# Sample streams' score tiles: the two halves of the keys side by side in place of two streams' tokens

## The chip, the cores and the metric

The kernel runs on one core of one Trainium2 chip. The metric is the device time of one execution in microseconds (us). A core has the engines PE (TensorE: matmuls and transposes, PEld is its weight load), DVE (VectorE), ACT (ScalarE), POOL (GpSimd) and SP (SyncE, which here only issues transfers); transfers run on 16 DMA engines shared by all queues.

## What is computed

Two layers over 512 prompt tokens and 8 sample streams of 16 new tokens each; layer 0 is stick-breaking attention, layer 1 gated linear attention. The change is in layer 0, in the attention of the sample streams. For one stream and one of 16 heads (head width 128) the keys are 512 cached ones followed by the stream's 16 new ones:

```python
z = einsum('bqhd,bkhd->bhqk', q, k) * SB_HEAD_DIM ** -0.5
mask = kpos[None, :] < qpos[:, None]
neg_log_keep = where(mask, softplus(z), 0.0)
between = cumsum(neg_log_keep, axis=3, reverse=True) - neg_log_keep
a = where(mask, exp(log_sigmoid(z) - between), 0.0)
o = einsum('bhqk,bkhd->bqhd', a, v)
```

So each weight is a sigmoid of its score times the product of (1 - sigmoid) over all later keys that the token may see: a running product over the keys from the last to the first.

## The kernel before

**The attention stage.** Heads are taken in 8 pairs. Per pair, q, k (head width on the partitions, tokens along the row) and v are fetched from scratch memory by `fetch_pair` (L959), two pairs held at a time. Three lanes work on them: two prompt lanes (one per head of the pair, four units of 128 queries per pair) and the sample lane (L1044), whose unit `u = (p, m)` is head pair p and the two streams 2m and 2m+1: 32 units in all.

**One unit of the sample lane.** `turned` transposes the cached keys of one stream (4 blocks for each head) on PE, and DVE or ACT copies them to `kt`. `scores` (L1076) fills a bank of 128 rows by 512 keys with four matmuls of 32 weight columns each, one for each row group j of 32 rows: group j is head j // 2 and stream j % 2, and its 32 rows are the 16 tokens of *both* streams, so that the 16 rows of the other stream are computed and never used. Four more matmuls of 32 columns put the new keys' scores in a second bank (`zn`, L1086); DVE adds a mask to it (L1087). `stick` (L939) takes two sigmoids of the 512 columns and two of the 32 on ACT (L945 to L949), and the running product on DVE as one scan over 544 columns (L952). DVE multiplies sigmoid and product (L1089 for 512 columns, L1091 for 32). `weigh` (L1095) transposes four blocks of weights (L1100) and the block of the new keys (L1103) into two banks; ACT copies the one (L1101), DVE the other (L1104). `mix` (L1107) multiplies by the values: 5 blocks of keys by 4 row groups, 20 matmuls. `leave` (L1121) transposes the result back and copies it to the pair's output. Each f32 matmul is two instructions in the trace.

**What sets the order.** PE's instructions run in the order in which they are written. That order comes from a planner at build time: a clock `pe["now"]` that advances by an estimate for each matmul, and a `Side` object (L276 to L343) whose `tick` is called between pieces of the large matrix products (`plain`, L650, and `share`, L696), which so fill PE between the lanes' steps. Each lane yields steps: an estimated wait, the number of PSUM banks of kind `tp` (4 exist here) and `z` (2 exist) that it needs free, and whether it is `tiled`, that is, uses matmuls of 32 weight columns. A step runs once its wait is over and its banks are free by the planner's own count, in which a `tp` bank is held for 2.2 us from when a step took it and a `z` bank for 3.0 us. In one tick the planner first collects the lanes that are due, runs those at an ordinary step, and then those of the same list that now stand at a tiled step, whose own wait is then not looked at again:

```python
due = [x for x in self.lanes if x[1][0] <= pe["now"]]
...
tiled = [x for x in due if x in self.lanes and x[1][2]]
if tiled and pe["now"] >= self.tiled_at + self.every:
    for x in tiled:
        if self.fits(x):
            self.run(x)
```

So `scores` of the next unit can be written right behind `weigh`, if the banks for both are free. The sample lane asks for: `turned` 2 `tp` (twice a unit), `scores` with the `mix` behind it 2 `tp` and 1 `z` (L1152; the first unit 1 `tp`), `leave` 1, `weigh` 2 (L1167), which is due 6.5 us of the planner's clock after `scores`. The other engines and the transfers are ordered by the framework; SP issues nearly all transfers, one after another, and a transfer that has to wait for its buffer holds up those behind it. Keys are fetched two units ahead into a ring of two buffers (`kc`), values one unit ahead into a ring of four (`vc`). `settle` (L980) hands a pair's output on to the output projection, and fetches the pair after the next.

Of the kernel before, what the change touches and what calls it, by code (L numbers as in the profile page):

```python
# [41 lines left out]
def hybrid_step_kernel(ctx: ExitStack, tc: tile.TileContext, A: dict, O: list):  # L42
# [22 lines left out]
    def block(x):  # L65

        pe["now"] += 0.11
        return x
# [840 lines left out]
    with tc.tile_pool(name="kp", bufs=2, reuse_waits="tile") as kp, \  # L909
# [10 lines left out]
        mask_n = at.tile([P, 32], F32, name="mask_n", bufs=1)  # L920
        nc.gpsimd.memset(mask_n, 0.0)
        for j in range(4):
            bi = j % 2
            q = mask_n[32 * j:32 * j + 32, :]
            nc.gpsimd.affine_select(out=q, in_=q, pattern=[[1, 32]], base=-16 * bi,
                                    channel_multiplier=0, compare_op=ALU.is_ge, fill=NEG)
            nc.gpsimd.affine_select(out=q, in_=q, pattern=[[-1, 32]], base=0,
                                    channel_multiplier=1, compare_op=ALU.is_gt, fill=NEG)
            if bi == 0:
                nc.gpsimd.affine_select(out=q, in_=q, pattern=[[0, 32]], base=15,  # L930
                                        channel_multiplier=-1, compare_op=ALU.is_ge, fill=NEG)
        zero_c = at.tile([P, 1], F32, name="zero_c", bufs=1)
        nc.gpsimd.memset(zero_c, 0.0)
        zeros = zero_c.to_broadcast([P, 544])
# [4 lines left out]
        def stick(kind, z, zn, n):  # L939

            w = n + (32 if zn is not None else 0)
            size = 544 if kind == "s" else 512
# [4 lines left out]
            if zn is not None:  # L947
                act(k1[:, n:w], zn, AF.Sigmoid, scale=-ZSCALE)  # L948
                act(s1[:, n:w], zn, AF.Sigmoid, scale=ZSCALE)  # L949
            nc.gpsimd.memset(k1[:, w:w + 1], 1.0)  # L950
            kr = k1[:, :w][:, ::-1]
            dve.tensor_tensor_scan(kr, kr, zeros[:, :w], 1.0, ALU.mult, ALU.add)  # L952
# [51 lines left out]
        def prompt_lane(hh):  # L1004
# [4 lines left out]
            def scores(u):  # L1009
# [6 lines left out]
                s1, k1 = stick("p", z[:, :n], None, n)  # L1016
# [27 lines left out]
        def sample_lane():  # L1044
# [4 lines left out]
            def cached(u, bi, s, tag, bufs, at=at):  # L1049
                p, m = units[u]  # L1050
                t = at.tile([P, 4, 256], F32, tag=tag, name=tag, bufs=bufs)
                src = A[s][0, 2 * m + bi].rearrange("(c p) h d -> p c (h d)", p=P)
                load(t, src[:, :, 256 * p:256 * p + 256])
                return t

            def fetch_k(u):
                if u < len(units):
                    for bi in range(2):
                        kc_t[u, bi] = cached(u, bi, "cache_sb_k", "kc", 2, kp)

            def fetch_v(u):
                if u < len(units):
                    vc_t[u] = [cached(u, bi, "cache_sb_v", "vc", 4) for bi in range(2)]

            def turned(kc):
                KTs = []
                for hh in range(2):
# [3 lines left out]
                    kt = at.tile([P, PAST], F32, tag="kt", name="kt", bufs=4)  # L1071
                    (nc.scalar.copy if hh else dve.tensor_copy)(kt, tp)
# [3 lines left out]
            def scores(u, KTs):  # L1076
                p, m = units[u]
                q, k = pairs[p][:2]
                tok = slice(NP + 32 * m, NP + 32 * m + 32)
                z, zn = bank("z"), bank("tp")  # L1080
                for j in range(4):
                    hh, bi = j // 2, j % 2
                    mm(z[32 * j:32 * j + 32, :], q[:, hh, tok], by(q[:, hh, tok], KTs[2 * bi + hh]), start=True, stop=True)  # L1083
                for j in range(4):
                    hh = j // 2
                    mm(zn[32 * j:32 * j + 32, :32], q[:, hh, tok], by(q[:, hh, tok], k[:, hh, tok]), start=True, stop=True)  # L1086
                dve.tensor_tensor(zn[:, :32], zn[:, :32], mask_n, op=ALU.add)  # L1087
                s1, k1 = stick("s", z, zn[:, :32], PAST)
# [915 lines left out]
```

## Time and profile before

| | |
|---|---|
| times of three runs | 2570.55, 2567.61, 2566.62 us; median 2567.61 |
| profiled execution | span 2566.7 us, as the fastest of the three runs |
| PE busy | 2450.5 us, 95% of the span |
| DVE / ACT / POOL busy | 1593.6 / 1015.8 / 163.6 us |
| mean granted TensorE clock | 0.979 |
| attention stage | about 936 to 1405 us of the span; the first `scores` of the sample lane at 949.6, the last at 1392.2 |

Times in a row of the trace are in us from the span's start; "mean ns" is the mean duration of one instruction. Matmuls are pipelined, so that what a group costs PE is read from the start of the group to the start of the next, not from its duration. "idle" names the time in which an engine stood before an instruction, and what ended it.

### The profile page before, as it was taken

To read this page: it belongs to the slowest core of one execution; us is meant where nothing else is said; L and a number is where in the kernel's file an instruction comes from. 1 tells how busy PE (TensorE), PEld (TensorE's weight loads), DVE (VectorE), ACT (ScalarE), POOL (GpSimd) and SP (SyncE) were. 2 spreads that over 40 slices of the span, in tenths; PEclk is the share of its full clock that TensorE was granted. 3 is DMA by queue.
4 is the path that set the end of the run, shared out by engine and by line. 5 is a ranking of instruction groups with operands and counts; after the bars stand their busy time and mean duration, and the time that the engine had idled before them with its cause. 6 is when DMAs were issued, how large, how long until landed. Compare 5 with 4: busy or idle time off the path is not lost.

```text
span 2566.7 us, 43490 instructions
## 1 busy us (share of the span) xinstructions
PE 2450.5 (95%) x17369; PEld 2156.7 (84%) x17369; DVE 1593.6 (62%) x2469; ACT 1015.8 (40%) x1794; POOL 163.6 (6%) x385
## 2 busy tenths in 40 slices
PE   6899999999999999999999989999999999979998
PEld 4589999999999998787777768999999988857776
DVE  5575655555566656666776577666767465555456
ACT  4332222222223335565444344333333464455223
POOL 0010000000000000000000000000000234342000
PEclk8999999999999999999999999999999999989999
DMA  9966666766663366766665763344444777785634
GB/s 341 330 200 222 214 205 215 231 214 195 211 197 117 121 210 204 232 214 221 215 220 176 238 197 120 107 121 138 116 115 117 209 228 246 226 281 192 207 119 144
DMA packets 452797, 502.06 MB, mean 196 GB/s; under 512 B 26090, under 2 KB 349810, under 8 KB 452466
## 3 DMA queue, kind: packets, MB, share of 16 engines
q1 hardware_dynamic: 429634, 435.55, 53.7%
q0 software_dynamic: 16048, 51.92, 6.1%
q10 hardware_dynamic: 6912, 11.80, 1.2%
q8 instruction: 137, 2.24, 0.4%
q14 instruction: 66, 0.54, 0.1%
HBM read 410.05 MB, written 89.13 MB: 194 GB/s over the span
## 4 chain that ended last, share of the span: by engine, by line
PE 76%; DMA 6%; DVE 6%; issue 2%; ACT 2%; POOL 1%; SPq 0%; ACTq 0%; POOLq 0%; DVEq 0%
PE ps_mm L592 39%; PE ps_mm L696 10%; PE ps_mm L650 6%; PE ps_mm L367 3%; PE ps_tp L1070 2%; PE ps_tp L1526 2%; PE ps_mm L516 1%; PE ps_tp L1038 1%; DMA gv<-kr 1%; PE ps_z L1014 1%; PE ps_z L180 1%; PE ps_mm L1975 1%; DVE wl L135 1%; PE ps_z L1083 1%; PE ps_tp L1115 1%
## 5 line engine op out<-in xcount | busy, mean ns | idle before, releaser
L592 PE MATMUL ps_mm<-sums,wh 128*128 128x320 f32 x2752 | 616.6, 312 | 3.8 <-ACT wh L134 3.8
L592 PEld LDWEIGHTS ps_mm<-sums,wh 128*128 128x128 f32 x2752 | 460.6, 189 | 12.9 <-issue 7.4
L592 PE MATMUL ps_mm<-h,wh 128*128 128x320 f32 x2064 | 462.5, 312 | 3.4 <-DVE u L598 3.4
L592 PE MATMUL ps_mm<-sums,wl 128*128 128x320 f32 x1376 | 427.1, 310 | 1.4 <-DVE wl L135 1.4
L135 DVE TENSOR_TENSOR wl<-wr,wh 128x1024 fp32r<-128x1024 f32 x194 | 237.2, 1224 | 241.2 <-ACT wh L134 234.8
L592 PEld LDWEIGHTS ps_mm<-h,wh 128*128 128x128 f32 x2064 | 343.6, 188 | 19.3 <-issue 13.3
L134 ACT CAST wh<-wb 128x1024 fp32r<-128x1024 f32 x170 | 178.4, 1049 | 426.6 <-PE ps_mm L592 368.6
L134 ACT CAST wh<-wr 128x1024 fp32r<-128x1024 f32 x194 | 203.6, 1050 | 335.5 <-PE ps_mm L592 185.6
L592 PE MATMUL ps_mm<-h,wl 128*128 128x320 f32 x1032 | 319.2, 309 | 0.0
L650 PE MATMUL ps_mm<-h,wh 128*128 128x320 f32 x1152 | 269.1, 321 | 8.6 <-ACT wh L134 4.1
L592 PEld LDWEIGHTS ps_mm<-sums,wl 128*128 128x128 f32 x1376 | 259.7, 189 | 1.9 <-DVE wl L135 1.9
L135 DVE TENSOR_TENSOR wl<-wb,wh 128x1024 fp32r<-128x1024 f32 x170 | 207.8, 1222 | 60.8 <-ACT wh L134 60.4
L650 PEld LDWEIGHTS ps_mm<-h,wh 128*128 128x128 f32 x1152 | 196.1, 192 | 25.6 <-issue 12.2
L696 PE MATMUL ps_mm<-wh,ogh 128*128 128x512 f32 x460 | 199.5, 434 | 5.6 <-DVE y L701 2.6
L592 PEld LDWEIGHTS ps_mm<-h,wl 128*128 128x128 f32 x1032 | 194.0, 188 | 0.0
L696 PE MATMUL ps_mm<-wh,ogl 128*128 128x512 f32 x460 | 181.5, 395 | 0.4 <-DVE ogl L135 0.4
L650 PE MATMUL ps_mm<-h,wl 128*128 128x320 f32 x576 | 180.8, 314 | 1.0 <-DVE wl L135 1.0
L696 PE MATMUL ps_mm<-wl,ogh 128*128 128x512 f32 x460 | 181.3, 394 | 0.0
L696 PEld LDWEIGHTS ps_mm<-wh,ogh 128*128 128x128 f32 x460 | 87.3, 190 | 33.4 <-issue 16.5
L650 PEld LDWEIGHTS ps_mm<-h,wl 128*128 128x128 f32 x576 | 110.6, 192 | 1.7 <-DVE wl L135 1.7
L952 DVE TENSOR_TENSOR_SCAN k<-k,zero_c 128x544 f32<-128x544 f32 (+4 forms) x96 | 93.3, 976 | 29.3 <-ACT k L948 16.6
L696 PEld LDWEIGHTS ps_mm<-wh,ogl 128*128 128x128 f32 x460 | 86.8, 189 | 20.7 <-DVE ogl L135 0.9
(352 smaller groups left out, 3773.3 us busy)
## 6 DMA issues: line engine op xcount, KB each, us to landing
ar<-in_w_ada_dram SPq DMA_DIRECT2D x160, 512.0 KB
wb<-in_sb_w_in_dram SPq DMA_DIRECT2D x82, 512.0 KB
kc<-in_cache_sb_k_dram SPq DMA_DIRECT2D x64, 512.0 KB
vc<-in_cache_sb_v_dram SPq DMA_DIRECT2D x64, 512.0 KB
wr<-in_gla_w_in_dram SPq DMA_DIRECT2D x51, 512.0 KB
wb<-in_gla_w_in_dram SPq DMA_DIRECT2D x45, 512.0 KB
wr<-in_sb_w_in_dram SPq DMA_DIRECT2D x44, 512.0 KB
ar<-in_w_ada_dram SPq DMA_DIRECT2D x64, 256.0 KB
```

The source lines that it names most:

```text
L134: nc.scalar.copy(hi, x)
L135: (e or dve).tensor_tensor(lo, x, hi.bitcast(F32), op=ALU.subtract)
L180: mm(acc[32 * q:32 * q + 32, :w], cT[:, kt + m, :], by(cT[:, kt + m, :], rs[m // each][:, m % each, q, :]), start=kt + m == 0, stop=kt + m ...
L367: mm(acc[a], l[:, c], by(l[:, c], r[:, k2, :]), start=kt == k0 and first, stop=kt == k0 + nk - 1 and last)
L516: mm(acc[a], l, by(l, r[:, e, :]), start=j == 0 and e == 0 and begun, stop=j == 7 and e == 1 and last)
L592: mm(acc, l[:, k, :], by(l[:, k, :], r), start=start and k == 0 and first, stop=k == 7 and last, skip_group_check=True)
L650: mm(acc[nt], l[:, k, :], by(l[:, k, :], r), start=k0 == 8 and k == 0 and first, stop=k0 == 0 and k == 7 and last)
L696: mm(acc, l, by(l, r[:, e, :]), start=i == 0 and e == 0 and first, stop=i == 1 and e == 1 and last)
L952: dve.tensor_tensor_scan(kr, kr, zeros[:, :w], 1.0, ALU.mult, ALU.add)
L1014: mm(z[:, :n], q[:, hh, qs], by(q[:, hh, qs], k[:, hh, :n]), start=True, stop=True)
L1070: turn_block(tp[:, P * c:P * c + P], block(kc[:, c, P * hh:P * hh + P]), ident)
L1526: mm(out, l[a], by(l[a], r[b]), start=start and n == 0, stop=stop and n == 2, skip_group_check=True)
```

## The change

In a row group of 32 rows there is now one stream and one head: rows 0 to 15 are its 16 tokens against the first 256 cached keys, rows 16 to 31 the same tokens against the last 256 and the new keys. The score tile has 256 columns of cached keys and 16 of new ones, in one bank.

- `q_one` (new tile) holds for both heads and all 8 streams 16 columns of zeros, the 16 query columns, and 16 of zeros. With the window that begins at the queries a matmul writes rows 0 to 15 and adds zero to rows 16 to 31; with the window that begins 16 earlier, the reverse. Scores are 8 matmuls of 256 columns (4 groups by 2 halves, added up in the bank) in place of 4 of 512. `fetch_q` loads `q_one` from the q scratch: two transfers of 64 KB for each pair, 128 partitions by 8 runs of 64 bytes each, the first at the start of the lane, the others behind the `scores` of a pair's last unit.
- The new keys' scores are 4 matmuls of 16 columns (before: 32), written beside the others in the same bank; their mask is 16 columns wide and lets rows 16 to 31 alone through.
- `stick` is two sigmoids of 272 columns and one scan over 272.
- The running product of the earlier half lacks the factor of the later half. A `stream_shuffle` brings each row's partner's product to it (one column), a `tensor_scalar` with the two columns of `later` turns it into 1 for the later half, and the product with the sigmoid becomes a `scalar_tensor_tensor` over 256 columns with that factor.
- The new keys' weights are written by two small multiplies (one for each stream) in place of one.
- `weigh` transposes 2 + 1 blocks into one bank, and ACT alone copies it (384 columns), to a fixed tile `aT_s`. `mix` has the same 20 matmuls; its 32 weight columns are windows that begin at row 0 or 16 of a group.
- In the planner: `scores` with `mix` asks for 1 `tp` in place of 2 (the first unit for none), `weigh` for 1 in place of 2, and is due 6.0 us after `scores` in place of 6.5.
- At the start of the stage, POOL's masks change (12 selects in place of 10), and it clears `q_one` and 16 columns of `aT_s`.

```diff
+        q_one = at.tile([P, 2, NB, 3 * NT], F32, name="q_one", bufs=1)
+        nc.gpsimd.memset(q_one, 0.0)
+        aT_s = at.tile([P, 3 * P + NT], F32, name="aT_s", bufs=1)
...
-            w = n + (32 if zn is not None else 0)
-            size = 544 if kind == "s" else 512
+            size = PAST // 2 + NT if kind == "s" else 512
...
-            if zn is not None:
-                act(k1[:, n:w], zn, AF.Sigmoid, scale=-ZSCALE)
-                act(s1[:, n:w], zn, AF.Sigmoid, scale=ZSCALE)
...
+            def fetch_q(p):
+                for hh in range(2):
+                    load(q_one[:, hh, :, NT:2 * NT], q_d[p][:, hh, NP:].rearrange("d (b t) -> d b t", b=NB))
...
-                z, zn = bank("z"), bank("tp")
-                for j in range(4):
-                    hh, bi = j // 2, j % 2
-                    mm(z[32 * j:32 * j + 32, :], q[:, hh, tok], by(q[:, hh, tok], KTs[2 * bi + hh]), start=True, stop=True)
-                for j in range(4):
-                    hh = j // 2
-                    mm(zn[32 * j:32 * j + 32, :32], q[:, hh, tok], by(q[:, hh, tok], k[:, hh, tok]), start=True, stop=True)
-                dve.tensor_tensor(zn[:, :32], zn[:, :32], mask_n, op=ALU.add)
-                s1, k1 = stick("s", z, zn[:, :32], PAST)
-                dve.tensor_tensor(s1[:, :PAST], s1[:, :PAST], k1[:, 1:PAST + 1], op=ALU.mult)
+                z = bank("z")
+                for n in range(2):
+                    for j in range(4):
+                        bi, hh = j // 2, j % 2
+                        l = q_one[:, hh, 2 * m + bi, NT - NT * n:3 * NT - NT * n]
+                        mm(z[32 * j:32 * j + 32, :256], l, by(l, KTs[j][:, n]), start=n == 0, stop=n == 1)
+                for j in range(4):
+                    bi, hh = j // 2, j % 2
+                    t0 = NP + NT * (2 * m + bi)
+                    l = q[:, hh, t0 - NT:t0 + NT]
+                    mm(z[32 * j:32 * j + 32, 256:272], l, by(l, k[:, hh, t0:t0 + NT]), start=True, stop=True)
+                dve.tensor_tensor(z[:, 256:272], z[:, 256:272], mask_n, op=ALU.add)
+                s1, k1 = stick("s", z[:, :272], 272)
+                w = at.tile([P, 1], F32, tag="w", name="w")
+                dve.stream_shuffle(w, k1[:, 0:1], [(r + 16) % 32 for r in range(32)])
+                dve.tensor_scalar(w, w, later[:, 1:2], later[:, 0:1], op0=ALU.mult, op1=ALU.add)
+                dve.scalar_tensor_tensor(s1[:, :256], s1[:, :256], w, k1[:, 1:257], op0=ALU.mult, op1=ALU.mult)
...
-                aT = at.tile([P, 5, P], F32, tag="aTs", name="aT", bufs=1)
                 tp = bank("tp")
-                for c in range(4):
+                for c in range(2):
                     turn_block(tp[:, P * c:P * c + P], block(s1[:, P * c:P * c + P]), ident)
-                nc.scalar.copy(aT[:, :4, :], tp.rearrange("p (b t) -> p b t", t=P))
-                tp = bank("tp")
-                turn_block(tp[:, :P], block(an), ident)
-                dve.tensor_copy(aT[:, 4, :], tp[:, :P])
-                made[u] = aT
+                turn_block(tp[:, 2 * P:3 * P], block(an), ident)
+                nc.scalar.copy(aT_s[:, :3 * P], tp[:, :3 * P])
+                made[u] = aT_s
...
             fetch_k(0)
+            fetch_q(0)
             fetch_v(0)
...
-                yield step(1.6, tp=1 if left or not u else 2, z=1, tiled=True)
+                yield step(1.6, tp=0 if left or not u else 1, z=1, tiled=True)
                 scores(u, KTs)
+                if m == 3 and p + 1 < NPAIR:
+                    fetch_q(p + 1)
...
-                yield step(max(0.5, made[u][2] + 6.5 - pe["now"]), tp=2)
+                yield step(max(0.5, made[u][2] + 6.0 - pe["now"]), tp=1)
```

More of the change, by code (lines that the diff above doesn't have):

```diff
@@ L1047, in sample_lane, with fetch_k @@
             made, kc_t, vc_t = {}, {}, {}
-            def cached(u, bi, s, tag, bufs, at=at):
+            def fetch_k(u):
+                if u >= len(units):
+                    return
                 p, m = units[u]
[L1051 to L1059, printed above, removed]
-            def fetch_v(u):
-                if u < len(units):
-                    vc_t[u] = [cached(u, bi, "cache_sb_v", "vc", 4) for bi in range(2)]
+                for bi in range(2):
+                    src = A["cache_sb_k"][0, 2 * m + bi].rearrange("(c p) h d -> p c (h d)", p=P)
+                    kc = kc_t[u, bi] = kp.tile([P, 4, 256], F32, tag="kc", name="kc")
+                    load(kc, src[:, :, 256 * p:256 * p + 256])
+            def fetch_q(p):
+                for hh in range(2):
+                    load(q_one[:, hh, :, NT:2 * NT], q_d[p][:, hh, NP:].rearrange("d (b t) -> d b t", b=NB))
+            def fetch_v(u):
+                if u >= len(units):
+                    return
+                p, m = units[u]
+                vc_t[u] = []
+                for bi in range(2):
+                    t = at.tile([P, 4, 256], F32, tag="vc", name="vc", bufs=4)
+                    src = A["cache_sb_v"][0, 2 * m + bi].rearrange("(c p) h d -> p c (h d)", p=P)
+                    load(t, src[:, :, 256 * p:256 * p + 256])
+                    vc_t[u].append(t)
             def turned(kc):
@@ L1070, in turned @@
                         turn_block(tp[:, P * c:P * c + P], block(kc[:, c, P * hh:P * hh + P]), ident)
-                    kt = at.tile([P, PAST], F32, tag="kt", name="kt", bufs=4)
-                    (nc.scalar.copy if hh else dve.tensor_copy)(kt, tp)
+                    kt = at.tile([P, 2, 256], F32, tag="kt", name="kt", bufs=4)
+                    (nc.scalar.copy if hh else dve.tensor_copy)(kt, tp.rearrange("p (s n) -> p s n", s=2))
                     KTs.append(kt)
@@ L1111, in mix @@
                     for j in range(4):
-                        hh, bi = j // 2, j % 2
+                        bi, hh = j // 2, j % 2
                         hc = slice(P * hh, P * hh + P)
                         rhs = V[bi][:, kb, hc] if kb < 4 else v[:, 4, hc]
-                        mm(o[32 * j:32 * j + 32, :P], aT[:, kb, 32 * j:32 * j + 32], by(aT[:, kb, 32 * j:32 * j + 32], rhs),
-                           start=kb == 0, stop=kb == 4)
+                        c0 = 32 * j + (P * (kb % 2) + NT * (kb // 2) if kb < 4 else 2 * P + NT)
+                        l = aT[:, c0:c0 + 32]
+                        mm(o[32 * j:32 * j + 32, :P], l, by(l, rhs), start=kb == 0, stop=kb == 4)
                 osb = at.tile([P, P], F32, tag="osb", name="osb")
```

39 lines of the change are left out of this document (21 added, 18 removed).

## The prediction

> **What bounds the kernel now.** I read the page first, then windows over the attention stage, then what PE waited for there.
>
> ```profile
> span 2566.7 us, 43490 instructions
> PE 2450.5 (95%) x17369; PEld 2156.7 (84%) x17369; DVE 1593.6 (62%) x2469; ACT 1015.8 (40%) x1794; POOL 163.6 (6%) x385
> PE 76%; DMA 6%; DVE 6%; issue 2%; ACT 2%; POOL 1%; SPq 0%; ACTq 0%; POOLq 0%; DVEq 0%
> ```
>
> ```profile
> 1000.00:1100.00 100.00, 93.84 (x919) 78.40 (x918) 67.44 (x140) 56.14 (x136) 1.81 (x24) 0.98 0.69 224
> 1100.00:1200.00 100.00, 100.00 (x856) 80.90 (x854) 63.66 (x127) 58.68 (x139) 1.86 (x23) 1.00 0.67 222
> 1200.00:1300.00 100.00, 97.23 (x865) 76.72 (x864) 75.61 (x149) 52.05 (x123) 1.79 (x23) 1.00 0.69 228
> ```
>
> ```profile
> PE ps_tp L1031 <- DVE s L1017: 5.4, 4, 2.7
> PE ps_tp L1070 <- DMA kc<-in_cache_sb_k_dram: 2.9, 1, 2.9
> PE ps_mm L696 <- ACT ogh L134: 2.3, 1, 2.3
> ```
>
> In a row of windows the first number after the length is PE's busy time, then PEld, DVE, ACT and POOL, the granted clock, the DMA share and GB/s. In the stage that the change touches, PE is busy 94 to 100 us of 100 at a clock of 0.98 to 1.00, DVE 64 to 76, ACT 52 to 59. The last fence has the three longest groups of PE's waits in 935 to 1410 us (total, times, longest): 5.4 us behind the prompt lanes' products on DVE, once 2.9 for keys, once 2.3 at the hand-over to `share`. So the stage is PE's own work written one after another, since `plain` and `share` fill what the lanes leave. Halving ACT's and DVE's work on the sample tiles, the larger part of the edit, hardly reaches the end; what PE no longer does counts in full, and so does each new wait of PE.
>
> **Transposes of the weights.** One `weigh` on PE, each row with its start first:
>
> ```profile
> 1255.00 0.60 PE L1100 MATMUL ps_tp<-ident,s 128*128 128x128 f32 x4
> 1255.44 0.27 PE L1103 MATMUL ps_tp<-ident,a_new 128*128 128x128 f32 x1
> ```
>
> Four transposes take 1255.44 - 1255.00 = 0.44 us, 0.11 each. Two are gone in each of 32 units: 64 x 0.11 = **-7.0 us**, on PE's path.
>
> **Scores and mix.** The block that follows it:
>
> ```profile
> 1257.93 1.06 PE L1083 MATMUL ps_z<-kt,q 128*32 128x512 f32 x8
> 1258.81 0.24 PE L1086 MATMUL ps_tp<-k,q 128*32 128x32 f32 x8
> 1258.87 1.06 PE L1115 MATMUL ps_tp<-vc,aT 128*32 128x128 f32 x32
> 1259.75 0.40 PE L1115 MATMUL ps_tp<-v,aT 128*32 128x128 f32 x8
> ```
>
> Eight instructions of 512 columns take 1258.81 - 1257.93 = 0.88 us; 32 instructions of `mix` with 128 columns, as many columns in all, also take 0.88. Four times the instructions cost nothing more, so 16 of 256 take 0.88 too: 0. The new keys' eight take 0.06; with 16 columns they lie between 0.03 and 0.06, so 0 to -1.0 us over 32 units; I take the middle, **-0.5**. `mix` keeps its 20 matmuls.
>
> The Trainium skill speaks against this: its page TensorEngine Tiling (Array Packing), section Instruction Overhead, gives each matmul some 60 cycles, and lets one with a free size of 1 take as long as one of 60. By it, and by the 2.4 GHz of the Trainium skill's page TensorE: Matmul & The Clock Gate (its table of figures), 8 more instructions would cost an estimated 8 x 60 / 2.4 = 200 ns a unit, 6.4 us in all, and the time would be 2568.4. The two equal blocks of 0.88 us above do not bear it out for groups in turn on four column tiles.
>
> **ACT and DVE.**
>
> ```profile
> L952 DVE TENSOR_TENSOR_SCAN k<-k,zero_c 128x544 f32<-128x544 f32 x32 | 41.3, 1289 | 16.7 <-ACT k L948 16.6
> L1089 DVE TENSOR_TENSOR s<-s,k 128x512 f32<-128x512 f32 x32 | 21.8, 682 | 0.0
> L952 DVE TENSOR_TENSOR_SCAN k<-k,zero_c 128x256 f32<-128x256 f32 x16 | 10.9, 685 | 1.8 <-ACT k L945 1.7
> L1017 DVE TENSOR_TENSOR s<-s,k 128x256 f32<-128x256 f32 x16 | 6.7, 422 | 0.8
> L1104 DVE COPY aT<-ps_tp 128x128 f32<-128x128 f32 x31 | 8.8, 285 | 7.7 <-PE ps_tp L1103 7.7
> L1091 DVE TENSOR_TENSOR a_new<-s,k 128x32 f32<-128x32 f32 x32 | 5.9, 185 | 0.0
> L945 ACT ACTIVATE k<-ps_z 128x512 f32<-128x512 f32 x48 | 28.8, 600 | 28.8 <-PE ps_tp L1086 17.7 <-DVE ps_z L1015 9.3 <-PE ps_z L1083 1.6
> ```
>
> DVE a unit: the scan falls from 1289 ns to a little over the 685 of 256 columns (some 720), the product from 682 to some 450 (422 for 256 columns, more for a second factor), the copy of 285 goes. Added are a second `a_new` (185), the shuffle and the small `tensor_scalar`. No row shows a shuffle; below it the least it can be is near nothing, above it the 422 ns of a product of 256 columns; I take 185 for each of the two, as the smallest row here. Sum: -570 -230 -285 + 3 x 185 = -0.5 us, 17 us over the stage (between -0.8 and -0.3 a unit). ACT saves two fifths of two sigmoids of 600 ns and the two small ones, near 1 us a unit. All this lies beside PE. It counts where PE waited for DVE: of the 5.4 us behind L1017 between 0 and all; I take **-1.5**, since most of that queue is the prompt lanes' own. The mask is now added before the sigmoids, so ACT stands at its head until DVE comes; casts of weights and copies of `kt` queue behind it. The near 1 us that it saves covers that; without this cover `turned` would wait for its bank.
>
> **The planner's order.** With one bank less asked for, `scores` will mostly be written right behind `weigh`, where it now mostly stands some 3 us later (1255.00 and 1257.93 above). Then `mix` comes 1 us behind `weigh` and can catch ACT's copy unfinished. One such place today:
>
> ```profile
> 996.60 1.06 PE L1083 MATMUL ps_z<-kt,q 128*32 128x512 f32 x8
> 997.48 0.24 PE L1086 MATMUL ps_tp<-k,q 128*32 128x32 f32 x8
> 997.76 1.08 PE L1115 MATMUL ps_tp<-vc,aT 128*32 128x128 f32 x32
> ```
>
> ```profile
> PE ps_tp L1115 <- ACT aT L1101: 1.1, 2, 0.6
> ```
>
> From L1086 to `mix` 0.28 us pass in place of 0.06. I count about 10 of 32 units so today; for 21 more, 0 to 0.22 each is 0 to +4.6. The second row (two waits, 1.1 us in all over the stage) puts the mean well under the bound, and the copy is shorter: **+1.1**. On the gain side, from 1060 to 1080 the lanes run without a large product to fill PE:
>
> ```profile
> 1060.00:1070.00 10.00, 7.41 (x94) 5.32 (x93) 8.47 (x23) 6.11 (x22) 0.30 (x3) 1.00 0.92 298
> 1070.00:1080.00 10.00, 7.25 (x39) 4.67 (x42) 7.83 (x15) 5.17 (x11) 0.23 (x3) 0.94 0.74 243
> ```
>
> In the first row 2.6 us are lost; the second holds the hand-over to `share`, which stays. A faster sample lane leaves more of the gates' products for this place: 0 to -2.6, I take **-1.5**.
>
> **The start.** Here the edit costs.
>
> ```profile
> 951.65 0.38 PE L1031 MATMUL ps_tp<-ident,s 128*128 128x128 f32 x2
> ...
> 953.49 0.31 PE L650 MATMUL ps_mm<-h,wl 128*128 128x320 f32 x1
> 956.68 1.94 PE L1070 MATMUL ps_tp<-ident,kc 128*128 128x128 f32 x8 [2.89 <-DMA kc<-in_cache_sb_k_dram]
> ```
>
> ```profile
> 953.40:956.70 3.30, 0.41 (x4) 0.18 (x2) 0.94 (x3) 0.00 (x0) 0.13 (x2) 0.87 1.11 359
> 956.70:963.40 6.70, 6.70 (x28) 6.58 (x29) 2.11 (x3) 2.92 (x6) 0.00 (x0) 0.56 0.80 262
> ```
>
> The second unit's keys land at 956.7, with the DMA engines full (share 1.11). PE waits 2.89 us, then runs at a clock of 0.56 for 6.7 us, which costs 6.7 x 0.44 = 2.9 more. By the planner's own count the large products from L1031 to 953.5 stand ahead of `turned` because three of four banks were held: one by the first `scores`, two by L1031. Now `scores` takes none, `turned` comes directly behind L1031, and 953.49 - 951.65 = 1.8 us of work moves behind the wait: +1.8. And `fetch_q` puts two transfers ahead of the values and keys on SP. The nearest is a load of 128 partitions by 9 runs of 64 bytes:
>
> ```profile
> 1420.57 0.43 SPq L71 DMA_DIRECT2D xp<-in_c_sample_dram  x1
> ```
>
> ```profile
> 1424.02 0.27 DVE L1222 COPY c<-xp 128x144 f32<-128x144 f32 x1
> ```
>
> ```profile
> 1420.57:1424.02 3.45, 2.43 (x11) 1.69 (x9) 3.45 (x5) 1.21 (x2) 0.00 (x0) 1.00 0.36 68
> ```
>
> It landed within 3.45 us, at a DMA share of 0.36 that four bias loads shared: at most 1.24 us of all 16 engines, near nothing at least. Two are 0 to 2.5; I take +2.0. If POOL clears `q_one` late, SP stands there with the value loads behind it, under cover of the transfers already queued. The start together: **+3.8** (0 to +6).
>
> The other seven `fetch_q` are issued behind a pair's last `scores` and needed at the next, a unit later:
>
> ```profile
> L1083 PE MATMUL ps_z<-kt,q x256: 592/617/1062, 949.6 to 1392.7; 128*32 128x512 f32 x128
> ```
>
> 32 units in 949.6 to 1392.7 are (1392.7 - 949.6) / 31 = 14.3 us each; 3.45 us for one load and 1.24 for the second fit. On SP they wait for that `scores`; behind them stands `fetch_v`, which waits for the `mix` just after it in any case: 0.
>
> **Sum.** -7.0 - 0.5 - 1.5 + 1.1 - 1.5 + 3.8 = -5.6. The profiled span of 2566.7 gives 2561.1; it equals the fastest of the runs shown (2566.62), and the median lies 0.9 above: **2562.0**.
>
> **Rivals.**
>
> *The order gains more than it costs.* All of PE's waits behind L1017 go, the lanes' bare stretch is filled, and the start pays for its order alone: -7.5 - 5.4 - 2.6 + 1.1 + 1.8 = -12.6, with the span and the 0.9: 2555.0. For it: DVE is at 8.47 of 10 in that stretch. Against: the waits are few and sit at the hand-over of pairs.
>
> *The start and `mix` eat it.* +6 and +2 against -7.5: 2568.1, no change. For it: both costs are read off above; against: they need their upper halves together.
>
> *More instructions in `scores` do cost.* At the price of the new keys' eight (0.06 us) 8 more a unit are 32 x 0.06 = +1.9: 2563.9. The Trainium skill's section Instruction Overhead, in TensorEngine Tiling (Array Packing), states this rule.
>
> *Slower: the keys come late at the turns of pairs.* A faster sample lane (now 14.3 us a unit) asks for its 2 MB sooner, while the next pair's q, k, v load and the DMA share stands at 0.92 (1060 to 1070). A miss costs what the one at the start does, 2.9 + 2.9 = 5.8 us. One gives 2567.8; from two on it decides: -5.6 + 11.6 = +6.0, 2573.6. For it: keys are asked for only when a buffer comes free. Against: there is one miss in the whole stage now, and the mean share is 0.67 to 0.69.
>
> **How the numbers follow.** Forecast 0.47, more gain 0.18, eaten 0.20, instruction price 0.03, late keys 0.12. 0.2% is 5.1 us, about what a measurement of this kernel can tell from no change, so faster begins at 2562.5. Of the forecast's own range (2558 to 2566) I put 0.28 below that and 0.19 above. Faster 0.28 + 0.18 = 0.46, same 0.19 + 0.20 + 0.03 = 0.42, slower 0.12. The range 2555 to 2571 takes in all but the late keys and the far end of the gain.
>
> **What would show it.** L1100's successor with 64 instructions and the new block's `scores` at 0.88 us bear out the PE terms; a longer block, the instruction price. A first wait for keys of over 4.5 us bears out the start. `scores` straight behind `weigh` in most units, and an earlier end of the sample lane with bare `share` behind it, bear out the order. Further waits of L1070's successor for keys, with a clock near 0.56 behind them, would make me wrong towards slower; a stage that shrinks by over 10 us, towards faster.

## The result

The changed kernel takes 2552.22 us (median; 2549.31 to 2556.43), the kernel before beside it 2567.11 (2564.66 to 2570.55). The ratio is 0.9947, with a 95% interval of 0.993 to 0.9963; two further measurements of the same pair, below, gave 0.9944 and 0.9948. The mean of the three, 0.9946, is 13.8 us of 2567.6. The forecast was 2562.0 with a range of 2555 to 2571: the sign is right, the size is not, and the rival "the order gains more than it costs" (2555.0) came closest. The profiled span fell from 2566.7 to 2554.7 us.

The page of the changed kernel:

```profile
span 2554.7 us, 43975 instructions
PE 2442.0 (96%) x17561; PEld 2159.4 (85%) x17561; DVE 1582.3 (62%) x2565; ACT 995.3 (39%) x1730; POOL 164.1 (6%) x390
PE 77%; DMA 7%; DVE 5%; ACT 3%; issue 2%; POOL 0%; SPq 0%; ACTq 0%; POOLq 0%; DVEq 0%
```

PE is still the engine that sets the end (77% of the chain of waits). DVE lost 11.3 us and ACT 20.5; PE lost only 8.5 busy us, less than the 12.0 by which the span shrank, so part of the gain is PE standing still less.

**Where the time went.** One length serves for all kernels below: "the stage", from the first product of the gates after the stage's weights arrive (L650) to the first transposes that follow a column of `share` (L1288 before, L1306 after). The timeline of PE, kernel before, then changed kernel:

```profile
936.69 0.53 PE L650 MATMUL ps_mm<-h,wh 128*128 128x320 f32 x2 [1.65 <-ACT wh L134]
...
1052.41 0.31 PE L650 MATMUL ps_mm<-h,wl 128*128 128x320 f32 x1
...
1072.92 0.48 PE L696 MATMUL ps_mm<-wh,ogh 128*128 128x512 f32 x1
...
1433.22 0.60 PE L1288 MATMUL ps_tp<-ident,y 128*128 128x128 f32 x4
```

```profile
936.70 0.53 PE L650 MATMUL ps_mm<-h,wh 128*128 128x320 f32 x2 [1.72 <-ACT wh L134]
...
1057.52 0.31 PE L650 MATMUL ps_mm<-h,wl 128*128 128x320 f32 x1
...
1067.19 0.48 PE L696 MATMUL ps_mm<-wh,ogh 128*128 128x512 f32 x1
...
1423.00 0.60 PE L1306 MATMUL ps_tp<-ident,y 128*128 128x128 f32 x4
```

The stage went from 1433.22 - 936.69 = 496.5 to 1423.00 - 936.70 = 486.3 us; two more profiles of the changed kernel gave 482.8 and 485.5 (mean 484.9, so -11.6). The stage has two parts. Up to the first product of `share` it went from 1072.92 - 936.69 = 136.2 to 130.5 us (128.6 and 130.3 in the two others; mean 129.8, so -6.4); behind it from 360.3 to 355.8 us (354.2 and 355.2; mean 355.1, so -5.2). In both kernels 8 of the 32 `weigh` stand in the first part and 24 in the second. At the 0.22 us that each spares (below) the transposes account for 1.8 us of the first and 5.3 of the second, so by these profiles all that the order gains in the stage lies ahead of `share`.

From the last row to the end of the span PE's instructions stand in the same order in both kernels, one by one. Yet this rest took 1133.5 us before and 1131.7, 1129.5 and 1129.1 in the changed kernel, 3.4 us less in the mean. Why is open; in the profiles of the kernels below it takes 1128 to 1138 us, so a difference of times of that size need not come from the stage. The second and third row of each timeline give the stretch in which the lanes run without a large product: 1072.92 - 1052.41 = 20.5 us before, 1067.19 - 1057.52 = 9.7 after.

The same windows as in the prediction, changed kernel (after the length: PE, PEld, DVE, ACT, POOL busy, granted clock, DMA share, GB/s):

```profile
1000.00:1100.00 100.00, 96.38 (x1024) 82.57 (x1026) 64.76 (x163) 51.28 (x118) 1.70 (x22) 0.98 0.77 248
1100.00:1200.00 100.00, 99.86 (x1000) 81.53 (x992) 68.28 (x168) 56.98 (x132) 1.83 (x24) 1.00 0.80 250
1200.00:1300.00 100.00, 99.36 (x975) 81.08 (x968) 74.71 (x181) 49.49 (x116) 1.84 (x24) 1.00 0.78 251
```

PE's gaps in the first and the third hundred (6.2 and 2.8 us before) shrank to 3.6 and 0.6. What they were is in PE's waits from 935 to 1410 us, changed kernel (in all, times, longest):

```profile
PE ps_z L1093 <- DMA q_one<-qd: 5.7, 1, 5.7
PE ps_tp L1131 <- ACT aT_s L1118: 2.3, 4, 0.8
PE ps_mm L650 <- ACT wh L134: 1.7, 1, 1.7
PE ps_tp L1079 <- DMA kc<-in_cache_sb_k_dram: 1.2, 1, 1.2
PE ps_tp L1032 <- DVE s L1018: 0.9, 1, 0.9
PE ps_mm L696 <- DVE y L701: 0.7, 2, 0.4
PE ps_mm L696 <- ACT ogh L134: 0.4, 1, 0.4
PE ps_tp L1079 <- DVE kt L1081: 0.4, 1, 0.4
PE ps_mm L696 <- DVE ogl L135: 0.3, 1, 0.3
```

Without the two for a transfer these are 6.7 us; the same sum before is 13.5, of which 5.4 behind the prompt lanes' products (now 0.9) and 2.3 + 0.4 at the hand-over to `share` (now 0.4 + 0.3). In place of the one wait for keys (2.9) stand a new one for `q_one` (5.7) and a smaller one for keys (1.2). The latter is at the second unit of a pair, in the stretch without a large product; one of the two other profiles has it too (1.22), the other has none:

```profile
1064.55 1.09 PE L1079 MATMUL ps_tp<-ident,kc 128*128 128x128 f32 x8 [1.24 <-DMA kc<-in_cache_sb_k_dram]
```

One unit of the sample lane in the changed kernel, PE's timeline:

```profile
1050.14 0.38 PE L1116 MATMUL ps_tp<-ident,s 128*128 128x128 f32 x2
1050.36 0.27 PE L1117 MATMUL ps_tp<-ident,a_new 128*128 128x128 f32 x1
1050.56 1.07 PE L1093 MATMUL ps_z<-kt,q_one 128*32 128x256 f32 x16
1051.45 0.23 PE L1098 MATMUL ps_z<-k,q 128*32 128x16 f32 x8
1051.51 1.06 PE L1131 MATMUL ps_tp<-vc,aT_s 128*32 128x128 f32 x32
```

Two transposes in 0.22 us; 16 instructions of 256 columns in 1051.45 - 1050.56 = 0.89 us, where 8 of 512 took 0.88; the new keys' eight still 0.06, though they have 16 columns in place of 32. And the order: `weigh` (L1116), the next unit's `scores` (L1093) and `mix` (L1131) with nothing between them. In the written order `scores` stands straight behind `weigh` in 29 of 31 places, in 11 of 31 before (in two of these with a small step of a prompt lane between).

The added and changed groups of DVE and ACT, changed kernel, 930 to 1410 us:

```profile
L953 DVE TENSOR_TENSOR_SCAN k<-k,zero_c 128x272 f32<-128x272 f32 x32 | 23.2, 724 | 13.3 <-ACT k L949 13.3
L1104 DVE SCALAR_TENSOR_TENSOR s<-s,w,k 128x256 f32<-128x256 f32 x32 | 15.3, 479 | 0.3
L1109 DVE TENSOR_TENSOR a_new<-s,k 64x16 f32<-64x16 f32 x64 | 10.6, 165 | 0.4
L1103 DVE TENSOR_SCALAR w<-w,later 128x1 f32<-128x1 f32 x32 | 8.7, 273 | 1.0
L1102 DVE STREAM_SHUFFLE w<-k 128x1 f32<-128x1 f32 x32 | 4.9, 152 | 0.0
```

### The profile page after: what moved, and what is told of

Same layout as the page of the kernel before. It is cut to its first block, busy times and chain, and to the rows that moved or that the text cites. A ratio compares the mean times of both kernels' runs of the same rounds, so it can differ in the third digit from the quotient of the medians.

```text
span 2554.7 us, 43975 instructions
## 1 busy us (share of the span) xinstructions
PE 2442.0 (96%) x17561; PEld 2159.4 (85%) x17561; DVE 1582.3 (62%) x2565; ACT 995.3 (39%) x1730; POOL 164.1 (6%) x390
## 4 chain that ended last, share of the span: by engine, by line
PE 77%; DMA 7%; DVE 5%; ACT 3%; issue 2%; POOL 0%; SPq 0%; ACTq 0%; POOLq 0%; DVEq 0%
PE ps_mm L592 39%; PE ps_mm L696 10%; PE ps_mm L650 7%; PE ps_mm L367 3%; PE ps_tp L1079 2%; PE ps_tp L1544 2%; DMA gv<-kr 1%; PE ps_mm L516 1%; PE ps_tp L1131 1%; PE ps_tp L1039 1%; PE ps_z L1015 1%; PE ps_z L180 1%; PE ps_mm L1993 1%; PE ps_z L1093 1%; PE ps_z L222 1%
## 5 line engine op out<-in xcount | busy, mean ns | idle before, releaser
L650 PE MATMUL ps_mm<-h,wh 128*128 128x320 f32 x1152 | 268.8, 321 | 10.2 <-ACT wh L134 5.8
L650 PEld LDWEIGHTS ps_mm<-h,wh 128*128 128x128 f32 x1152 | 195.6, 192 | 27.2 <-issue 12.3
L650 PE MATMUL ps_mm<-h,wl 128*128 128x320 f32 x576 | 180.2, 313 | 0.4 <-DVE wl L135 0.4
L650 PEld LDWEIGHTS ps_mm<-h,wl 128*128 128x128 f32 x576 | 110.1, 191 | 0.8 <-DVE wl L135 0.8
L516 PE MATMUL ps_mm<-wh,h 128*128 128x512 f32 x252 | 93.5, 433 | 4.3 <-ACT h L134 1.9
```

Of the source, the lines that this page charges most:

```text
L516: mm(acc[a], l, by(l, r[:, e, :]), start=j == 0 and e == 0 and begun, stop=j == 7 and e == 1 and last)
L650: mm(acc[nt], l[:, k, :], by(l[:, k, :], r), start=k0 == 8 and k == 0 and first, stop=k0 == 0 and k == 7 and last)
```

## The experiments

Theory A: what the change gains beyond its transposes comes from the order in which PE's work is written (the planner asks for fewer banks, so `scores` follows `weigh` at once and the sample lane moves faster). Theory B: it comes from the work that DVE and ACT are spared. All results in one table. "Against the changed kernel" is (ratio - 0.9946) x 2567.6; the stage and PE's waits (those of 935 to 1410 us that are not for a transfer) come from one profile each, read as above.

| kernel | ratio to before (95%) | against the changed kernel, us | stage, us | PE's waits, us |
|---|---|---|---|---|
| before | 1 | +13.8 | 496.5 | 13.5 |
| changed, three times | 0.9947, 0.9944, 0.9948 | 0 | 486.3, 482.8, 485.5 | 6.7, 8.1, 6.4 |
| old_steps | 0.9994 (0.9979 to 1.001) | +12.3 | (503.9) | 15.6 |
| before_new_steps | 1.0006 (0.9992 to 1.002) | +15.4 | 500.2 | 12.6 |
| more_turns | 0.9978 (0.9965 to 0.9991) | +8.2 | 495.5 | 8.7 |
| more_dve_act | 0.9946 (0.9929 to 0.9963) | 0.0 | 486.0 | 6.3 |
| old_scores | 0.9968 (0.9956 to 0.998) | +5.6 | 491.0 | 7.7 |
| old_weigh | 0.9986 (0.9976 to 0.9995) | +10.3 | 487.4 | 9.2 |
| old_early | 1.001 (0.9996 to 1.0024) | +16.4 | 495.1 | 14.9 |
| old_late | 0.9978 (0.9967 to 0.999) | +8.2 | 490.1 | 7.7 |
| late_slow | 0.9967 (0.9955 to 0.9979) | +5.4 | 487.9 | 5.9 |
| late_apart | 0.9962 (0.9948 to 0.9976) | +4.1 | 489.7 | 5.9 |
| q_first | 0.9956 (0.9939 to 0.9973) | +2.6 | 485.4 | 4.4 |
| first_later | 0.9961 (0.9946 to 0.9977) | +3.9 | 485.1 | 8.5 |
| q_first_keys_later | 0.9946 (0.9928 to 0.9965) | 0.0 | 483.1 | 7.7 |

An interval is 2.4 to 4.8 us to either side, so differences under some 4 us are not told from nothing. The stage is read from one profile for each kernel but the changed one, whose three differ by 3.5 us. The profiled execution of old_steps was the longest of its kernel (2579.67 us against a median of 2566.89), so its stage is put in brackets and not used.

**The old order under the new computation** (old_steps):

```diff
-                yield step(1.6, tp=0 if left or not u else 1, z=1, tiled=True)
+                yield step(1.6, tp=1 if left or not u else 2, z=1, tiled=True)
...
-                yield step(max(0.5, made[u][2] + 6.0 - pe["now"]), tp=1)
+                yield step(max(0.5, made[u][2] + 6.5 - pe["now"]), tp=2)
```

> The changed kernel with the planner's three old numbers: `scores` asks for 1 or 2 banks again, `weigh` for 2 and 6.5. Compute edits alone remain. Theory A (what the change gains beyond its transposes comes from the order of PE's work): 5 to 6 us are lost against the changed kernel, about 2558, and PE's waits behind the prompt lanes' products (5.4 us before, 0.9 after) and at the hand-over to `share` (2.75 before, 0.7 after) come back. Theory B (it comes from DVE and ACT having less to do): within 2 us of the changed kernel, about 2552, and the waits stay short.

2566.89 us: 12 us of the 13.8 are gone, twice what theory A expected. The computation alone, with its transposes, cannot be told from the kernel before (0.9994). PE's waits are back at 15.6 us, and the stretch without a large product is 33.3 us long (20.5 before). By the 0.45 us for each us of stretch that old_early gives below, these 12.8 us would cost an estimated 5.8, most of what the spared transposes save. B falls here: DVE and ACT have the new, smaller work in this kernel.

**The new order under the old computation** (before_new_steps; the same three numbers, in the kernel before).

> The kernel before with the planner's three new numbers alone: `scores` asks for 0 or 1 banks and `weigh` for 1 and 6.0, while they still take 1 or 2 and 2. Theory A: most of the order's gain without any compute edit, 3 to 6 us faster than before, about 2562; the sample lane ends some 35 us earlier than 1392.7. Theory B: no gain; the banks that are taken and not asked for make PE wait, 2567 to 2571.

No gain. Up to the first product of `share` the stage is 127.7 us long (136.2 before, with one unit's `scores` more in it), and behind it 372.5 (360.3 before). The stretch without a large product is short here too, but `mix` now comes right behind `weigh` and finds the weights not yet copied. PE's waits in this kernel, 935 to 1410 us:

```profile
PE ps_tp L1115 <- ACT aT L1101: 5.7, 4, 2.3
PE ps_tp L1070 <- DMA kc<-in_cache_sb_k_dram: 4.9, 1, 4.9
PE ps_tp L1115 <- DVE aT L1104: 2.0, 1, 2.0
```

7.7 us at `mix` (1.8 before, 2.3 in the changed kernel), 6.2 of them behind the first product of `share`. This is the cost that the prediction named for the new order (0 to +4.6), met in full and more where `scores` takes one bank and `weigh` two that the planner isn't asked for. So the order and the computation need each other: neither alone can be told from the kernel before.

**The transposes alone** (more_turns):

```diff
                 turn_block(tp[:, 2 * P:3 * P], block(an), ident)
+                for c in range(2):
+                    turn_block(tp[:, 3 * P:], s1[:, P * c:P * c + P], ident)
                 nc.scalar.copy(aT_s[:, :3 * P], tp[:, :3 * P])
```

> The changed kernel with two more transposes in each `weigh`, which nothing reads; the order is that of the changed kernel, since the planner isn't told of them. If the transposes lie on PE's path, as the prediction's first term has it, 64 x 0.11 = +7.0 us, about 2559. If PE has slack beside them (it waits for DVE or a load right after), +2 or less.

+8.2 us, 10.6 in the stage (495.5 against the mean of 484.9). The row of the added transposes shows 64 instructions (busy us and mean ns are pipelined durations; from start to start two take 0.22 us as above):

```profile
L1119 PE MATMUL ps_tp<-ident,s 128*128 128x128 f32 x64 | 12.2, 273 | 0.0
```

64 x 0.11 = 7.0 lies within what was measured: the first term stands. PE's other waits are a little longer too (8.7 us against a mean of 7.1).

**The work of DVE and ACT** (more_dve_act): two more sigmoids and one more scan for each sample tile, on a tile that nothing reads.

```diff
+            if kind == "s":
+                act(more, z, AF.Sigmoid, scale=ZSCALE)
             act(k1[:, :n], z, AF.Sigmoid, scale=-ZSCALE)
             act(s1[:, :n], z, AF.Sigmoid, scale=ZSCALE)
+            if kind == "s":
+                act(more, z, AF.Sigmoid, scale=ZSCALE)
...
+            if kind == "s":
+                kr = more[:, ::-1]
+                dve.tensor_tensor_scan(kr, kr, zeros[:, :272], 1.0, ALU.mult, ALU.add)
```

> The changed kernel with DVE's and ACT's work on a sample tile about as long as before: two more sigmoids of 272 columns and one more scan of 272, on a tile that nothing reads; PE's order is that of the changed kernel. By the page ACT fell by 20.5 us and DVE by 11.3. Theory A (order and PE's own work): 0 to +2 us against the changed kernel. Theory B (relief of DVE and ACT): +5 or more, with PE waiting behind the prompt lanes' products or for the weights at `mix`.

No difference (0.9946 and 0.9946; stage 486.0), although the page has the two engines back where they were:

```profile
PE 2441.7 (96%) x17561; PEld 2160.0 (85%) x17561; DVE 1600.6 (63%) x2597; ACT 1012.8 (40%) x1794; POOL 164.4 (6%) x390
```

Halving the sigmoids and the scan, the larger part of the edit, is worth nothing here, and B is out as it was put. What stays spared in this kernel are the shorter copies behind `weigh` (one of 384 columns on ACT, none on DVE); it is at them that PE waits in before_new_steps.

**Which of the planner's numbers** (old_scores and old_weigh: the first or the second line of old_steps alone), beside the changed kernel once more (after_again).

> The changed kernel once more, unchanged, beside the three others of this call: the yardstick for them. 13 to 14 us faster than before (0.9947 so far), about 2553 to 2555.

> The changed kernel in which only the step of `scores` asks for the old number of banks (1 or 2 in place of 0 or 1); `weigh` keeps 1 and 6.0. With both numbers old the stage from the first product of the gates to the first `turn` grew from 486.3 to 503.9 us. If what counts is that `scores` comes right behind `weigh`, this edit alone brings most of it back: 8 to 14 us slower than the changed kernel, near 2565, and PE waits again behind the prompt lanes' products (8.9 us with both, 0.9 without). If it is the request of `weigh`, under 4.

> The changed kernel in which only `weigh` asks for the old 2 banks, at 6.5 after `scores`; `scores` keeps 0 or 1. If the place of `scores` decides: under 4 us slower than the changed kernel, though 32 units that are 0.5 longer by the planner's count (14 us of the lane's 400) make the sample lane end later. If the earlier `weigh` decides: 8 to 14 us slower.

+5.6 and +10.3: either request undoes a good part, and not, as expected, the one of `scores` alone. The written orders say why: with either of them `scores` stands behind `weigh` at once in only 8 or 9 of 31 places, since more banks must be free at the same moment. The 6.0 in place of 6.5 does nothing: with 6.5 and one bank the program that is built is the same.

Not all of old_weigh's +10.3 is in the stage, which is 2.5 us longer in its profile (487.4 against 484.9). Its twelve runs have a granted clock of 0.976 to 0.978, 0.977 in the mean; after_again beside it has 0.980, and so has the kernel before. Within the twelve runs of old_steps the time falls by some 1.7 us for each 0.001 of that clock, so an estimated 4 to 5 us of the 10.3 go with the clock. Why it is lower is open.

**Where the order gains** (old_early: the three old numbers for the first nine units, up to the first product of `share`; old_late: from the tenth on).

```diff
+                old = u < 9
-                yield step(1.6, tp=0 if left or not u else 1, z=1, tiled=True)
+                yield step(1.6, tp=(1 if left or not u else 2) - (0 if old else 1), z=1, tiled=True)
...
-                yield step(max(0.5, made[u][2] + 6.0 - pe["now"]), tp=1)
+                yield step(max(0.5, made[u][2] + (6.5 if old else 6.0) - pe["now"]), tp=2 if old else 1)
```

> The changed kernel with the three old numbers of the planner for the first nine units of the sample lane only, so up to the first product of `share`. In the written order the lane then has 6 units' `scores` ahead of the last product of the gates (8 in the changed kernel, 7 before), and the stretch without large products holds 3 units in place of 1; 23 later units keep the new numbers. With all three old everywhere the ratio to before was 0.9994, in the changed kernel 0.9945, 13 us apart. If the order's gain is made in that stretch and at the hand-over to `share`: 8 to 13 us slower than the changed kernel, near 2562. If it is made beside `share`: 0 to 4 us slower.

> The counterpart: the three old numbers from the tenth unit on; the first nine keep the new ones, and the stretch without large products stays at one unit. `scores` stands straight behind `weigh` in 9 of 31 places (29 in the changed kernel, 11 before). If the order's gain is made in the stretch and at the hand-over: 0 to 4 us slower than the changed kernel, near 2553. If it is made beside `share`, where scores and weights follow each other: 8 to 13 us slower.

+16.4 and +8.2; their sum is more than old_steps cost, which has both (+12.3), so they do not simply add up. Of the 16.4 the stage shows 10.2; old_early's runs too have a clock of 0.977 in the mean, and 0.979 the kernel before beside it. In old_early the stretch is 32.5 us long; the timeline of PE, old_early:

```profile
1045.25 0.31 PE L650 MATMUL ps_mm<-h,wl 128*128 128x320 f32 x1
...
1077.74 0.47 PE L696 MATMUL ps_mm<-wh,ogh 128*128 128x512 f32 x1
```

and among PE's waits of old_early those that the change had made small are large again:

```profile
PE ps_tp L1131 <- ACT aT_s L1118: 3.6, 5, 1.2
PE ps_tp L1032 <- DVE s L1018: 3.5, 3, 1.4
PE ps_mm L696 <- ACT ogh L134: 2.5, 1, 2.5
```

The stretch grew by 32.5 - 9.7 = 22.8 us and the stage by 495.1 - 484.9 = 10.2, or 0.45 us for each us of stretch, with 14.9 - 7.1 = 7.8 us more of PE's waits, the hand-over's 2.5 (0.4 in the changed kernel) among them. old_late is the other part: the stretch stays at 9.9 us and PE's waits at 7.7, yet the stage is 5.2 us longer. The timeline of PE, old_late:

```profile
934.27 0.53 PE L650 MATMUL ps_mm<-h,wh 128*128 128x320 f32 x2 [1.63 <-ACT wh L134]
...
1066.68 0.48 PE L696 MATMUL ps_mm<-wh,ogh 128*128 128x512 f32 x1
...
1424.41 0.60 PE L1307 MATMUL ps_tp<-ident,y 128*128 128x128 f32 x4
```

Up to the first product of `share`, where PE's instructions stand in the order of the changed kernel, it is 132.4 us long (mean there 129.8), so 2.6 of the 5.2 cannot come from the old numbers. Behind it it is 357.7 (355.1), +2.7. And the rest of the span, again in the same order, is 1137.5 us long against 1130.1.

**The part beside `share`** (late_slow and late_apart, with the changed kernel as after_third):

```diff
-                yield step(max(0.5, made[u][2] + 6.0 - pe["now"]), tp=1)
+                yield step(max(0.5, made[u][2] + (6.0 if u < 9 else 11.75) - pe["now"]), tp=1)
```

```diff
+                late = u >= 9
+                if late:
+                    yield step(1.6)
-                yield step(1.6, tp=0 if left or not u else 1, z=1, tiled=True)
+                yield step(0.0 if late else 1.6, tp=0 if left or not u else 1, z=1, tiled=True)
```

> The changed kernel in which `weigh` is due 11.75 after `scores` in place of 6.0 from the tenth unit on; the banks asked for stay. In the written order `scores` still stands straight behind `weigh` in 29 of 31 places, but 1008 products of `share` (128x512) stand beside the sample lane, 837 in the changed kernel, 957 before, 987 with the old numbers from the tenth unit on. If that lane's pace makes the gain beside `share`: 8 to 12 us slower than the changed kernel. If it is that `scores` and `weigh` stand together: within 3.

> The opposite: from the tenth unit on `scores` comes at least 1.6 after `weigh`, so that the two stand apart (together in 6 of 31 places), while the banks asked for stay new and the lane is slowed less: 906 products of `share` beside it. If standing together makes the gain beside `share`: 6 to 9 us slower than the changed kernel, as with the old numbers there. If the lane's pace does: (906 - 837) / (987 - 837) of that, 3 to 4 us.

> The changed kernel unchanged, the yardstick for the two others of this call: 0.9945 of before, about 2553.

+5.4 and +4.1, in the stage +3.0 and +4.8, each with 3 to 4 us of uncertainty. If the pace makes the gain, 8 to 12 were expected of late_slow and 3 to 4 of late_apart: the first costs less, and the second is near it but not told from nothing. If standing together makes it, within 3 and 6 to 9 were expected, and neither is met. The profiles do not bear out a loss beside `share`. Up to its first product, in the order of the changed kernel, late_slow and late_apart are 132.2 and 133.1 us long (129.8 there); behind it 355.6 and 356.7 (355.1), +0.6 and +1.6; the rest of the span, in the same order again, takes 1134.3 and 1135.4 us (1130.1). So where old_late, late_slow and late_apart lose what their times show stays open, and that the order gains anything beside `share` is not shown.

**The start** (q_first, first_later, q_first_keys_later). In the changed kernel the first `scores` waits:

```profile
949.38 0.31 PE L650 MATMUL ps_mm<-h,wl 128*128 128x320 f32 x1
955.41 2.26 PE L1093 MATMUL ps_z<-kt,q_one 128*32 128x256 f32 x16 [5.72 <-DMA q_one<-qd]
957.08 0.66 PE L1098 MATMUL ps_z<-k,q 128*32 128x16 f32 x8
```

SP's own timeline shows the reason, three value loads ahead of `q_one` and keys behind it:

```profile
940.76 8.28 SPq L71 DMA_DIRECT2D vc<-in_cache_sb_v_dram  x3
949.13 2.77 SPq L71 DMA_DIRECT2D q_one<-qd  x2
951.99 2.79 SPq L71 DMA_DIRECT2D kc<-in_cache_sb_k_dram  x1
```

The first edit clears only what the load does not fill, which puts the load ahead of the values; the second lets the first `scores` wait on the planner's clock; the third is the first with a later `turned` of the second unit's keys.

```diff
-        nc.gpsimd.memset(q_one, 0.0)
+        for c in (slice(0, NT), slice(2 * NT, 3 * NT)):
+            nc.gpsimd.memset(q_one[:, :, :, c], 0.0)
```

```diff
-                yield step(1.6, tp=0 if left or not u else 1, z=1, tiled=True)
+                yield step(1.6 if u else 8.0, tp=0 if left or not u else 1, z=1, tiled=True)
```

```diff
-                        yield step(0.5, tp=2)
+                        yield step(0.5 if u or bi else 6.0, tp=2)
                         KTs += turned(kc_t.pop((u + 1, bi)))
```

> The changed kernel with only the two outer thirds of `q_one` cleared, so that its loads need not wait for the clearing and go onto SP ahead of the first values. The wait of 5.72 us of the first `scores` for `q_one` goes. If the start cost what the prediction gave it, 3.8 us, most of it returns: about 2548.5. If the wait for the second unit's keys (2.89 us before, with 2.9 more in the slower clock behind it) only comes back in its place: 0 to -2, about 2551.

> The changed kernel, whose first `scores` is due 8.0 after the last keys are turned in place of 1.6, so that products of the gates stand ahead of it while `q_one` travels. The wait of 4.7 to 5.7 us and the slower clock behind it go, but the lane starts later: 7 units ahead of the last gate product in place of 8. If the start is worth what the wait shows: 4 to 6 us faster than the changed kernel. If a late lane takes it back in the stretch without large products (2 units of it again): within 3.

> The kernel with only the outer thirds of `q_one` cleared (its load ahead of the values), and the second unit's keys are turned 6.0 after the first `scores` in place of 0.5, so that products of the gates run while these keys travel. The written order keeps 8 units ahead of the last gate product. Both waits at the start (5.72 for `q_one`, 4.66 for the keys when `q_one` came first) go: 3 to 6 us faster than the changed kernel, near 2547, if PE has other work there and a wait at the start costs its length; within 2 if the keys, asked for later by as much, are late at the next unit instead.

None is faster than the changed kernel. In q_first the wait only changes its name:

```profile
946.63 1.21 PE L1094 MATMUL ps_z<-kt,q_one 128*32 128x256 f32 x13 [0.37 <-DMA q_one<-qd]
...
954.07 1.94 PE L1080 MATMUL ps_tp<-ident,kc 128*128 128x128 f32 x8 [4.66 <-DMA kc<-in_cache_sb_k_dram]
```

In first_later PE waits for nothing at the start, but the lane is a unit behind, the stretch without large products is 23.3 us long, and in it PE waits 4.9 us for keys: the loss moves to that stretch. In q_first_keys_later the keys are waited for once more, 2.4 us; the stage of 483.1 is no shorter than the changed kernel's shortest. So no version here beats the changed kernel.

## Why the prediction was wrong in size

Step by step, with the profile's figure for the changed kernel against the one before:

| step | forecast, us | shown |
|---|---|---|
| transposes | -7.0 | -7.0 by the rows (0.22 a unit); 8.2 when put back |
| new keys' matmuls | -0.5 | 0: 0.06 us with 16 columns as with 32 |
| PE's waits behind the prompt lanes' products | -1.5 | -4.5 (5.4 to 0.9; 1.6 and 0.9 in the two other profiles) |
| `mix` behind `weigh` | +1.1 | +0.5 (1.1 + 0.7 to 2.3) |
| hand-over to `share` | 0 | -2.0 (2.3 + 0.4 to 0.4 + 0.3) |
| bare stretch filled | -1.5 | 20.5 to 9.7 us; most of its gain is in the two waits |
| start | +3.8 | +1.6 |
| keys at the turns of pairs | 0 | +1.2 (+1.2 and 0 in the two other profiles) |
| behind the stage | 0 | -3.4 in the mean, same order of PE |

Without a figure of its own for the stretch the rows of the stage come to -7.0 - 4.5 + 0.5 - 2.0 + 1.6 + 1.2 = -10.2, and the stage measured -11.6, within the 3.5 us by which its three profiles differ. The forecast also took the time to lie 0.9 us above the profiled span; the changed kernel's profiled run lies 2556.43 - 2554.7 = 1.7 above its own.

**Right.** The transposes lie on PE's path. 16 instructions of 256 columns cost no more than 8 of 512, so the price by the Trainium skill's TensorEngine Tiling (Array Packing), section Instruction Overhead (a fixed cost for each matmul), is not borne out for these groups: 0.89 us against 0.88. The new order does what was said, `scores` behind `weigh`, and the cost at `mix` is of the size given. Keys were late at the turn of one pair alone, by 1.2 us where the rival had 5.8 with the slower clock, and not in each profile. The other seven loads of `q_one` cost nothing: the one wait for `q_one` is the first. And DVE's and ACT's smaller work hardly reaches the end: more_dve_act puts it at nothing.

**Wrong: "ACT and DVE", the -1.5.** The waits behind L1017 were put down to the prompt lanes' own queue on DVE and expected to stay for the most part. They fell by 4.5 us, and not because DVE had less to do (more_dve_act leaves them at 0.5, old_early has 3.5 again): they arise where lanes run with no large product between their steps, and the order took most of that stretch away. The cause was read from the engine that the wait names; it lay in what PE had left to put in front of it. The same holds for "the hand-over to `share`, which stays": it fell by 2.0 and came back with the old order (2.5 in old_early).

**Wrong: "the bare stretch", the -1.5.** It was priced by PE's idle time in one window of 10 us (2.6 at most). The faster lane cut the stretch by 10.8 us; old_early shows 10.2 us of the stage for 22.8 us of stretch, 0.45 for each, so by that rate some 4.8 us with the waits in it.

**Beside `share`** the forecast saw no gain from the order, and the kernels before and after show none: behind the first product of `share` the stage is 5.2 us shorter, where the transposes give 5.3. That the old numbers there cost 8.2 us (2.7 of them in that part) is not explained by this, and stays open, as do the 3.4 us behind the stage.

**Mis-sized: the start, +3.8.** The displaced products and the two transfers were added to the wait for keys; in fact the wait for `q_one` took its place. The clock behind it, changed kernel:

```profile
955.40:962.10 6.70, 6.69 (x54) 5.74 (x55) 2.66 (x9) 1.71 (x5) 0.13 (x2) 0.75 0.95 301
```

The wait is 5.7 - 2.9 = 2.8 us longer, but the clock behind it is 0.75 where it was 0.56: 6.7 x 0.25 = 1.7 us lost in place of 2.9. Together +1.6. The price of the two transfers was too low: from their issue at 949.13 to the end of the wait 6.3 us pass, for which the prediction had 0 to 2.5.

## What to carry to other kernels

A bank that an edit frees can be worth more than the work it saves: here neither the computation alone nor the order alone could be told from nothing, and both together gave 13.8 us, of which some 3.4 stand behind the stage for a reason not known. So try a planner's requests and the edit separately and together. Waits of the bounding engine that cluster where it has nothing large to run are one item, not several: price the length of that stretch, not each wait by the engine that it names. And compare the stretches in which an edit changes no order as well: here they differed by 2 to 7 us between single profiles, as much as the smaller effects. A wait at the start of a stage whose DMA engines are full moves to the next load in the queue when it is removed.

## What was not expected of the hardware

- Two loads of 64 KB in runs of 64 bytes, issued behind three value loads, took 6.3 us from the first one's issue to the end of the wait (949.13 to 955.41), and in q_first, issued ahead of the values, 9.5 us to 946.63. SP's timeline, q_first:

```profile
937.10 7.39 SPq L71 DMA_DIRECT2D q_one<-qd  x2
944.59 1.86 SPq L71 DMA_DIRECT2D vc<-in_cache_sb_v_dram  x2
```

  SP spends 7.39 us on the two alone, and the values stand behind them. At the later pairs two such loads take SP about 1 us; SP's timeline, changed kernel:

```profile
1051.67 0.99 SPq L71 DMA_DIRECT2D q_one<-qd  x2
```

  So the short runs alone do not make the 7.39 us. The Trainium skill's DMA: Bandwidth & Descriptors, section Specifications, asks for transfers of at least 512 bytes for full rate; no run here shows what the short runs add to the time until the data are there.
- A `tensor_scalar` on one column with two scalars read from a tile takes 273 ns, more than the shuffle of the same column (152 ns); the forecast had 185 for each. None of it shows in the time.
- Eight matmuls of 16 columns take the 0.06 us that eight of 32 columns take.
